# First query, key and value slabs of a two-layer decoder trunk as seven block products in Strassen's way

## The chip, the cores and the metric

The kernel runs on one core of a Trainium2 chip. The core has a matrix engine (TensorE, PE in the profile; its weight loads are shown as PEld), a vector engine (VectorE, DVE), an activation engine (ScalarE, ACT), a general engine (GpSimd, POOL) and a sync engine (SyncE, SP) that issues most DMAs. Each engine takes its instructions in the order in which they stand in its queue and waits where one is not ready. The metric is the device time of one launch in microseconds; less is better.

## The reference

Two layers on 512 tokens of 1024 channels, all float32. Layer 0 is a convolution module, layer 1 differential attention; each is followed by a gated feed-forward part (`ffn`) and a per-layer-embedding gate (`ple`). The part that matters here is the start of layer 1:

```python
h = h + sigmoid(rms_norm(h, ple_norm_g) @ ple_w_gate) * (p @ ple_w_proj)   # in substance; end of layer 0
u = rms_norm(h, attn_norm_g)
qkv = u @ w_qkv                                  # [512,1024] @ [1024,3072]
q, k, v = jnp.split(qkv, 3, axis=-1)
q = rms_norm(q.reshape(B, S, N_HEADS, 2, HEAD_DIM), q_g) * (HEAD_DIM ** -0.5)
k = rms_norm(k.reshape(B, S, N_HEADS, 2, HEAD_DIM), k_g)
...
logits = jnp.einsum('bhcqd,bhckd->bhcqk', q_blk, k) + bias[None, :, None]
probs = softmax(where(dist >= 0, logits, -inf))
w = probs[:, :, 0] - lam * probs[:, :, 1]
o = w @ v
```

`bias` is a table of 32 values for each of 8 heads, looked up by distance (T5), and `lam` one number made of four short vectors.

## The kernel before

**Arithmetic.** A float32 product is made of three passes in a reduced format: each operand is split in a high part (`hi`, a cast on ACT) and what is left (`lo`, a subtraction on DVE or POOL), and `mm3` (L166 to L170) issues lo x hi, hi x hi and hi x lo into one accumulator. `weight` (L147 ff) loads one [128 x 1024] piece of weights by SP (tile `wraw`, 2 buffers), casts it on ACT (L161, tile `whi`) and subtracts on DVE (L163, tile `wlo`). Accumulators `mm` have 4 buffers in PSUM, `sc` (scores) 2, `tp` (transposes and small things) 2.

**Order.** The program is written in stages; the instructions of each engine are set in order by a scheduler, except where a region is put under a manual schedule: there the engine's instructions stand as the code has them. `issue_after` holds an instruction behind another one in the order.

**`ple`, the end of layer 0** (L1110 to L1135). Eight products (`sums`), each one 1024 x 128 weight piece times the 512 tokens: 24 matmuls of 128x512. The first two come ahead of the normaliser: `norm.diagonal` transposes the sum of squares on PE (L237), reduces on DVE (L198, L279), takes the power on POOL (L281), and multiplies the result into two diagonal matrices on DVE (L244, L245, L286). `norm.rows` spreads them over all rows on PE (L302) and copies the outcome to `rb` on ACT (L252). Then `gate` runs for each product: accumulator times `rb` on DVE (L1122), sigmoid on ACT (L1123), times `pp` and plus `h` on DVE (L1124, L1125), and `after` for that channel group, which is `Norm.chunk`: the split of `h` times the attention norm's gain into hi (ACT, L202) and lo (DVE, L203), tiles `A0` to `A7`, and the square (ACT, L222/L225) that POOL adds to `acc` (L226). The normaliser of attention itself is applied behind the matmuls, by a factor for each token, `rcol`.

**The bias table and lambda** (L1155 to L1182). `rl` and `oh` are loaded, two matmuls (L1164) give the table by distance, DVE copies it (L1165), an ACT-queue DMA stores it to DRAM (`scr`, L1167); `bias` loads a head's rows back on the same queue (L1171). Lambda is made from a few small instructions.

**Queries, keys and values.** The weight matrix is cut into six slabs of [1024 x 512] in the order of the table `QKV` (L87): four with the queries and keys of two heads each ("q") and two with the values of four heads ("v"). A slab has four weight pieces and four token blocks of 128; `tokens` (L1200) makes one token block with 8 channel groups x 3 = 24 matmuls of 128x512, the tokens as the stationary operand. So a slab has 96. For a "q" block `unit` follows: square and copy with `rcol` on ACT (L1233, L1234), reduce on DVE (L1236), two small steps and a multiply on POOL (L1239 to L1242); and a block later `unit_end`: four transposes on PE (L1248), copies on ACT (L1256, L1257), on POOL (L1261) and on DVE (L1264, L1266) into the tiles `C0` to `C5` that the scores read. `rcol` itself is made behind the first token block (L1208 to L1210). A "v" block is an ACT copy (L1226).

**Attention blocks.** Each head has four blocks of 128 queries, each in three stages: `stage_s` (scores of two components: matmuls L1297 and L1300, an added bias with a running minimum on DVE L1310, exponentials on ACT L1314, a combination on DVE), `stage_t` (transposes L1327) and `stage_a` (the product with the values L1340). `take` hands out as many as the third entry of the `QKV` row says, to be run between the matmuls of the later slabs. Four instructions of the value slab's loop store `h` to DRAM (`rest`, SP), and `pfeatures` and the first piece of the next `ple`'s projection weights are fetched in the first query slab.

Of the kernel before, what the change touches and what calls it, by code (L numbers as in the profile page):

```python
# [12 lines left out]
F32 = mybir.dt.float32  # L13
# [7 lines left out]
P = 128  # L21
# [65 lines left out]
QKV = (("q", 0, (0, 0, 0, 0)), ("v", 0, (1, 1, 1, 2)), ("q", 1, (1, 1, 1, 2)), ("q", 2, (1, 1, 2, 1)), ("v", 1, (1, 1, 2, 2)), ("q", 3, (1, 1, 1, 1)))  # L87
# [5 lines left out]
def trunk(ctx, tc, xT, xtok, pT, wts, diag, dww, vec, rel, onehot, lamv, out):  # L93
# [29 lines left out]
    def col(name, i=0):  # L123
        a, _ = VEC[name]
        return vt[:, a + i : a + i + 1]
# [1025 lines left out]
    ple(n2, pp, lambda m, cut: norm.chunk(m))  # L1151

# [13 lines left out]

    def bias(hd):
        b = sb([P, S], "bias", 2)  # L1170
        nc.scalar.dma_start(b, bass.AP(scr.tensor, scr.offset + hd * RW, [[1, P], [1, S]]))  # L1171
        return b
# [6 lines left out]
    V.tensor_reduce(out=lam[:, 0:2], in_=lv[:, 0:2], op=ALU.add, axis=AX.X)  # L1179
# [19 lines left out]

    def tokens(ws, tb, between=()):  # L1200
# [6 lines left out]
        if rcol[0] is None:  # L1207
            r = sb([P, 4], "rcol", 1)  # L1208
            V.tensor_copy(r, norm.columns())
            rcol[0] = r  # L1210
        return acc, rcol[0][:, tb : tb + 1]
# [11 lines left out]

    def unit(pair, ws, tb, between):

        if tb == 0:  # L1226
            qk[pair] = [sb([P, 2, S], f"C{i}", 2, F32R) for i in range(6)]

            for c in range(2):
                with tc.issue_after(n2.last.ins):  # L1230
                    G.memset(f(qk[pair][4 + c][HALVES[1 - c]]), 0.0)
        acc, r = tokens(ws, tb, between)
        q, sq = big(), wk()  # L1233
# [6 lines left out]
        G.tensor_tensor(rs, rs, mhalf, ALU.pow)  # L1240
        q3 = q.rearrange("p (g d) -> p g d", g=8)
        G.tensor_tensor(q3, q3, rs.unsqueeze(2).to_broadcast([P, 8, DH]), ALU.mult)  # L1242
        return pair, tb, q
# [133 lines left out]
    todo = [(hd, qb) for hd in range(NH) for qb in range(4)]  # L1377
    todo.append(todo.pop(todo.index((NH - 2, 3))))
# [23 lines left out]
    waiting = None  # L1402
    for what, at, pace in QKV:
        ws = slab(GLO if at > 0 else 0)
        for tb in range(4):
            between = take(pace[tb])
            between += [None] * (6 - len(between))
            if waiting:
                between.append(partial(unit_end, *waiting))
                waiting = None  # L1410
            if what == "v":
                values(at, ws, tb, between)
            else:
                waiting = unit(at, ws, tb, between)

            if (what, at, tb) == ("q", 0, 1):
                ph = pfeatures(1, [both(sb([P, 2, S], t, 1, F32R)) for t in ("B4", "B5")])
            elif (what, at, tb) == ("q", 0, 2):
# [4 lines left out]

            elif (what, at) == ("v", 0):
                for c in (2 * tb, 2 * tb + 1):
                    nc.sync.dma_start(rest[c], h[c])
# [9 lines left out]
    unit_end(*waiting)  # L1436
# [204 lines left out]
```

## Time and profile before

| | |
|---|---|
| median of three runs | 1237.09 us (1237.03 to 1237.67) |
| the profiled execution's own time | 1234.18 us |
| its span | 1232.3 us |
| granted clock of PE, mean | 1.0 |
| weights read | 159 loads of 512 KB by SP, 3.6 us each from issue to landing |
| span of `ple` and the first two slabs | 542.5 to 630.7 us |

The profile shows one execution. A row of its timeline has the start in us from the span's start, the duration in us, the engine, the line of the kernel, the operation, what it writes and reads, the shape, and how many such instructions run together; in brackets stands how long the engine was idle before it and what released it. A row without a bracket followed its predecessor at once or nearly so. A row with "q" behind the engine's name is a DMA issued on that engine's queue. In the windows, each row gives a stretch and each engine's busy time in it.

### The profile page before, as it was taken

What the parts mean: (1) busy time and instruction counts of PE and PEld (TensorE: products, weight loads), DVE (VectorE), ACT (ScalarE), POOL (GpSimd) and SP (SyncE); (2) the same over time, 40 slices, a digit from 0 to 9 for tenths busy, and PEclk for the clock granted to TensorE, in tenths of its full rate; (3) what the DMA queues carried; (4) which work ended last, traced back from release to release, by engine and by line L of the source; (5) the groups of instructions that cost most, each with busy time, mean ns of one, the idle gap of its engine ahead of it and who ended that gap; (6) DMA issues with size and microseconds to landing.
All of it is one profiled execution on the core that took longest, in us unless ns stands there. A gap on an engine that the chain in (4) does not pass through costs nothing.

```text
span 1232.3 us, 18295 instructions
## 1 busy us (share of the span) xinstructions
PE 1221.3 (99%) x7003; PEld 1071.1 (87%) x7003; DVE 876.0 (71%) x1254; ACT 629.4 (51%) x1107; POOL 483.5 (39%) x360
## 2 busy tenths in 40 slices
PE   9999999999999999999999999999999999999998
PEld 7888688889998899888788888888889998999887
DVE  5979866975895488547767876747956885587545
ACT  7564554533553355435667877744524552355432
POOL 1777722025560554143436635131026641562220
PEclk9999999999999999999999999999999999999999
DMA  8484233233333232334423331243243233233321
GB/s 325 147 306 158 70 92 101 90 111 120 87 102 120 89 102 71 101 105 155 140 85 106 94 97 32 75 131 89 87 132 104 86 120 109 83 101 89 105 97 69
DMA packets 49875, 138.18 MB, mean 112 GB/s; under 512 B 5715, under 2 KB 10835, under 8 KB 49788
## 3 DMA queue, kind: packets, MB, share of 16 engines
q1 hardware_dynamic: 47520, 133.45, 33.6%
q10 hardware_dynamic: 2268, 3.57, 0.9%
q8 instruction: 55, 0.90, 0.3%
q14 instruction: 32, 0.26, 0.1%
HBM read 130.68 MB, written 6.31 MB: 111 GB/s over the span
## 4 chain that ended last, share of the span: by engine, by line
PE 92%; DVE 3%; DMA 2%; ACT 1%; issue 1%; POOL 0%; SPq 0%; ACTq 0%; DVEq 0%; POOLq 0%
PE mm L168 28%; PE mm L169 28%; PE mm L170 28%; PE mm L1340 1%; PE sc L496 1%; DVE sc L554 1%; DMA wraw<-in_wts 1%; PE sc L1300 1%; PE tp L1327 1%; PE sc L1297 1%; PE tp L1248 1%; DMA h<-in_xT 0%; DVE wlo L163 0%; DMA po<-big 0%; PE tp L1370 0%
## 5 line engine op out<-in xcount | busy, mean ns | idle before, releaser
L161 ACT CAST whi<-wraw 128x1024 fp32r<-128x1024 f32 (+1 forms) x139 | 141.2, 1025 | 230.3 <-PE mm L170 107.3
L163 DVE TENSOR_TENSOR wlo<-wraw,whi 128x1024 fp32r<-128x1024 f32 (+1 forms) x130 | 164.3, 1269 | 62.7 <-ACT whi L161 62.3
L168 PE MATMUL mm<-A,wlo 128*128 128x512 f32 (+1 forms) x524 | 203.1, 388 | 1.3 <-DVE wlo L163 1.2
L169 PE MATMUL mm<-A,whi 128*128 128x512 f32 (+1 forms) x524 | 202.4, 386 | 0.0
L170 PE MATMUL mm<-A,whi 128*128 128x512 f32 (+1 forms) x524 | 198.9, 386 | 0.0
L168 PE MATMUL mm<-B,wlo 128*128 128x512 f32 x356 | 139.0, 390 | 0.0
L169 PE MATMUL mm<-B,whi 128*128 128x512 f32 x356 | 138.8, 390 | 0.0
L226 POOL TENSOR_TENSOR acc<-acc,wk 128x512 f32<-128x512 f32 x35 | 61.1, 1744 | 195.2 <-ACT wk L225 170.8
L170 PE MATMUL mm<-B,whi 128*128 128x512 f32 x356 | 137.4, 389 | 0.0
L169 PE MATMUL mm<-C,whi 128*128 128x256 f32 (+1 forms) x450 | 127.6, 283 | 0.0
L170 PE MATMUL mm<-C,whi 128*128 128x256 f32 (+1 forms) x450 | 127.5, 283 | 0.0
L168 PE MATMUL mm<-C,wlo 128*128 128x256 f32 (+1 forms) x450 | 127.5, 283 | 0.0
L921 DVE TENSOR_TENSOR wlo<-A,whi 128x1024 fp32r<-128x1024 f32 x60 | 107.3, 1797 | 19.4 <-ACT whi L920 19.2
L168 PEld LDWEIGHTS mm<-A,wlo 128*128 128x128 f32 x524 | 98.4, 188 | 21.9 <-DVE wlo L163 1.6
L170 PEld LDWEIGHTS mm<-A,whi 128*128 128x128 f32 x524 | 98.4, 188 | 20.0
L169 PEld LDWEIGHTS mm<-A,whi 128*128 128x128 f32 x524 | 98.5, 188 | 19.6
L920 ACT CAST whi<-A 128x1024 fp32r<-128x1024 f32 x60 | 62.8, 1047 | 56.0 <-PE mm L170 45.1
L930 POOL TENSOR_TENSOR A<-A 128x512 f32<-128x512 f32 x16 | 25.8, 1614 | 161.5 <-DMA A<-in_wts 155.8
L930 POOL TENSOR_TENSOR A<-wraw 128x512 f32<-128x512 f32 x16 | 23.1, 1443 | 166.2 <-DMA wraw<-in_wts 128.7
L168 PEld LDWEIGHTS mm<-C,wlo 128*128 128x128 f32 x450 | 86.4, 192 | 0.2
L169 PEld LDWEIGHTS mm<-C,whi 128*128 128x128 f32 x450 | 86.4, 192 | 0.2
L170 PEld LDWEIGHTS mm<-C,whi 128*128 128x128 f32 x450 | 86.4, 192 | 0.1
(388 smaller groups left out, 3109.9 us busy)
## 6 DMA issues: line engine op xcount, KB each, us to landing
wraw<-in_wts SPq DMA_DIRECT2D x159, 512.0 KB, 3.6
A<-in_wts SPq DMA_DIRECT2D x32, 512.0 KB, 3.6
wraw<-in_wts SPq DMA_DIRECT2D x16, 384.0 KB, 3.0
D<-in_diag SPq DMA_DIRECT2D x17, 256.0 KB, 5.2
C<-in_diag SPq DMA_DIRECT2D x16, 256.0 KB, 5.5
h<-in_xT SPq DMA_DIRECT2D x8, 256.0 KB, 4.5
B<-in_xtok SPq DMA_DIRECT2D x4, 512.0 KB, 7.0
rest<-h SPq DMA_DIRECT2D x8, 256.0 KB, 2.0
```

The source lines that it names most:

```text
L161: A.copy(hi[:, cut], raw[:, cut])
L163: eng.tensor_tensor(lo[:, cut], raw[:, cut], f(hi[:, cut]), ALU.subtract)
L168: T.matmul(acc, al, bh, start=first, stop=False, **kw)
L169: T.matmul(acc, ah, bh, start=False, stop=False, **kw)
L170: return T.matmul(acc, ah, bl, start=False, stop=last, **kw)
L226: self.last = self.eng.tensor_tensor(self.acc, self.acc, sq, ALU.add)
L496: last_tap[0] = T.matmul(acc[:, g * P : (g + 1) * P], w, ups[c][:, g, LEAD - m : LEAD - m + P], start=(m == 0), stop=(m == LAGS - 1),)
L554: last = V.scalar_tensor_tensor(sum_, tap(j), wt(c, j), sum_, ALU.mult, ALU.add)
L920: A.copy(hi, src)
L921: V.tensor_tensor(lo, src, f(hi), ALU.subtract)
L930: G.tensor_tensor(s[:, 0], r1[:, 0], r1[:, 1], ALU.add)
L1248: turned[0] = T.transpose(t[:, i * P : (i + 1) * P], q[:, i * P : (i + 1) * P], ident)
```

## The change

The first query slab and the first value slab are made together. With the tokens cut in two halves, the channels in two halves (k = 0 to 3 and 4 to 7) and the weights of the two slabs as columns, the product of two 2x2 block matrices takes seven block products instead of eight (Strassen's scheme in Winograd's form). The blocks of the tokens are A11, A12, A22 (parts of the tiles `A0` to `A7`) and four sums S1 to S4 of blocks; those of the weights are W11, W12, W21, W22 and sums. Each block product has two token blocks x 4 channel groups x 3 matmuls of 128x512 = 24, so seven make 168 where two slabs had 192.

- `token_sums` makes S1 to S4 for channel groups k and k + 4 from `h` times the gain, while `ple` runs, as channels 4 to 7 become ready: on POOL for the first three, on DVE for the last; hi and lo on ACT and DVE.
- `sums_of` makes the sums of weight blocks on POOL (128x1024 each, 8 of them); `form` casts a block or sum and subtracts its lo part on DVE.
- `block_pair` runs the products with PE under a manual schedule, combines them (U2, P1 and P5 in tiles `D0` to `D5`), and calls `unit_norm` and `unit_end` for the query blocks and the first attention blocks in the last two products.
- The bias table's matmuls and the first steps of lambda stand ahead of `ple` in the program instead of behind it. The stores of `h` to `rest` come before the block products; `pfeatures` and the projection weight move to the next query slab.
- The first eight attention blocks have another order, since the first half of the tokens is ready first.

```diff
-QKV = (("q", 0, (0, 0, 0, 0)), ("v", 0, (1, 1, 1, 2)), ("q", 1, (1, 1, 1, 2)), ("q", 2, (1, 1, 2, 1)), ("v", 1, (1, 1, 2, 2)), ("q", 3, (1, 1, 1, 1)))
+QKV = (("q", 0, ()), ("v", 0, ()), ("q", 1, (1, 1, 2, 2)), ("q", 2, (1, 1, 2, 1)), ("v", 1, (1, 1, 2, 2)), ("q", 3, (1, 1, 1, 1)))
...
-    ple(n2, pp, lambda m, cut: norm.chunk(m))
+    def token_sums(k, eng):
+        g1, g2 = col("attn_g", k), col("attn_g", k + 4)
+        u2 = big()
+        A.activation(u2, h[k + 4], AF.Copy, scale=g2)
+        t = sb([P, 4, HT], f"B{k % 2}", 1)
+        if eng is V:
+            V.scalar_tensor_tensor(t[:, 0], h[k][:, HT:], g1, u2[:, HT:], ALU.mult, ALU.add)
+            V.scalar_tensor_tensor(t[:, 1], h[k][:, :HT], g1, t[:, 0], ALU.mult, ALU.subtract)
+        else:
+            u1 = big()
+            A.activation(u1, h[k], AF.Copy, scale=g1)
+            G.tensor_tensor(t[:, 0], u1[:, HT:], u2[:, HT:], ALU.add)
+            G.tensor_tensor(t[:, 1], u1[:, :HT], t[:, 0], ALU.subtract)
+        last_sums[k] = eng.tensor_tensor(
+            t[:, 2:4], t[:, 1:2].to_broadcast([P, 2, HT]), u2.rearrange("p (j t) -> p j t", j=2), ALU.add)
...
+        for i, (hi, lo) in enumerate(parts):
+            last_mixed[0] = A.copy(hi, t[:, i * n : (i + 1) * n])
+        for i, (hi, lo) in enumerate(parts):
+            last_mixed[1] = V.tensor_tensor(lo, t[:, i * n : (i + 1) * n], f(hi), ALU.subtract)
...
+    def after_gate(m, cut):
+        norm.chunk(m)
+        if m > 3:
+            token_sums(m - 4, G if m < 7 else V)
+        at = {0: ("11", SLABS, ("B2", "B3")), 2: ("12", SLABS + 4, ("B6", "B7")), 3: ("21", SLABS + 2, ("B4", "B5"))}
+        if m in at:
+            n, i, tags = at[m]
+            load_block(n, i, [(t, 1) for t in tags])
+        if m == 2:
+            form("1", W["11"], homes=[("C2", "C3"), ("C0", "C1")])
+        if m == 3:
+            with tc.issue_after(last_pow[0].ins):
+                sums_of(W["11"], W["12"], W["11"], ALU.subtract)
...
+    def sums_of(out, a, b, op):
+        for o, x, y_ in zip(out, a, b):
+            G.tensor_tensor(o, x, y_, op)
...
+    ple(n2, pp, after_gate)
+    load_block("22", SLABS + 6, [("wraw", 2)] * 2)
...
+    for i, at in enumerate([(0, 0), (0, 1), (1, 0), (1, 1), (0, 2), (0, 3), (1, 2), (1, 3)]):
+        todo[i] = at
...
+        for c in range(NC):
+            nc.sync.dma_start(rest[c], h[c])
...
+        for j in range(2):
+            product(a[j], "A11", "1", j, True)
+            with tc.issue_after(last_mixed[0].ins):
+                A.copy(p1[j], a[j])
+        open_pair(0)
+        form("2", W["21"])
+        products(x, "A12", "2")
+        for j in range(2):
+            with tc.issue_after(last_mixed[1].ins):
+                V.tensor_tensor(p1[j], x[j], p1[j], ALU.add)
+        form("5", W["11"])
+        with tc.issue_after(last_sums[2].ins):
+            sums_of(W["11"], W["11"], W["22"], ALU.subtract)
+        with tc.issue_after(norm.last.ins):
+            sums_of(W["12"], W["22"], W["12"], ALU.subtract)
+        products(y_, "S1", "5", factors)
+        for j in range(2):
+            waiting.append(unit_norm(0, j, p1[j], r(j)))
+        for j in range(2):
+            p5.append(sb([P, S], f"D{2 + j}", 1))
+            A.activation(p5[j], y_[j], AF.Copy, scale=r(2 + j))
+        form("6", W["11"])
+        with tc.issue_after(last_q[0].ins):
+            sums_of(W["11"], W["11"], W["21"], ALU.add)
+        for j in range(2):
+            product(a[j], "S2", "6", j, False)
+            u2.append(sb([P, S], f"D{4 + j}", 1))
+            A.activation(u2[j], a[j], AF.Copy, scale=r(j))
+        form("3", W["22"], (last_r[0], last_r[0]))
+        val[0, 0] = sb([P, 2, S], "B0", 1)
+        two = ends()
+        for j in range(2):
+            product(y_[j], "S4", "3", j, False, [None, two[j]])
+            V.scalar_tensor_tensor(val[0, 0][:, j], y_[j], r(j), u2[j], ALU.mult, ALU.add)
+        form("7", W["12"])
+        val[0, 1] = sb([P, 2, S], "B1", 1)
+        for j in range(2):
+            product(a[j], "S3", "7", j, False, take(1))
+            V.scalar_tensor_tensor(val[0, 1][:, j], a[j], r(2 + j), p5[j], ALU.mult, ALU.add)
+        form("4", W["11"])
+        for j in range(2):
+            product(a[j], "A22", "4", j, False, take(1))
+            waiting.append(unit_norm(0, 2 + j, a[j], r(2 + j)))
+
+    with tc.manual_schedule(engines={T.engine}):
+        block_pair()
+    for what, at, pace in QKV[2:]:
...
```

`products` issues channel groups 0 to 2 of both token blocks first, then `then` (here `factors`, which makes `rcol`), then group 3 of both. The changed kernel's lines of interest: scores L1385 and L1388, minimum L1398, exponential L1402, `unit_end` transposes L1336, its passes on ACT L1344 and L1345, on POOL L1349, on DVE L1352 and L1354, query scaling on POOL L1327, L1328 and L1330, value combinations L1573 and L1578.

**Where instructions move: PE in `ple`.** PE's queue in the fourth product of `ple` before: the two spread matmuls (L302, into `tp`) stand among the first matmuls of the product into `mm_5254`.

```order
L168 MATMUL mm_5254<-A_768_4859,wlo_5250 128x512
L169 MATMUL mm_5254<-A_768_4859,whi_5249 128x512
L302 MATMUL tp_5181<-wk_5145,ones_70 128x512
L170 MATMUL mm_5254<-A_768_4859,whi_5249 128x512
L168 MATMUL mm_5254<-A_770_4865,wlo_5250 128x512
L302 MATMUL tp_5181<-wk_5147,ones_70 128x512
L169 MATMUL mm_5254<-A_770_4865,whi_5249 128x512
```

The same place in the changed kernel, at the end of the fourth product (`mm_5288`); the fifth is `mm_5336`.

```order
L168 MATMUL mm_5288<-A_806_5093,wlo_5284 128x512
L169 MATMUL mm_5288<-A_806_5093,whi_5283 128x512
L170 MATMUL mm_5288<-A_806_5093,whi_5283 128x512
L302 MATMUL tp_5199<-wk_5163,ones_70 128x512
L302 MATMUL tp_5199<-wk_5165,ones_70 128x512
L168 MATMUL mm_5336<-A_768_4859,wlo_5332 128x512
L169 MATMUL mm_5336<-A_768_4859,whi_5331 128x512
```

The spread has moved behind the fourth product's last matmul, directly ahead of the fifth product, whose accumulator is the buffer that the first gate reads. The transposes ahead of it (L237) have moved from 36 matmuls into `ple` to 77.

**ACT's queue in `ple`.** In the changed kernel the store of the bias table (`scr`) and two loads from it stand among the casts of weights (`whi`), ahead of the copy to `rb`; before, they stood behind all of `ple`.

```order
L161 CAST whi_5385<-wraw_5384 128x1024
L1237 DMA scr<-C_810_5104 8x640
L1252 DMA bias_5837<-scr 128x512
L161 CAST whi_5439<-wraw_5438 128x1024
L1252 DMA bias_5902<-scr 128x512
L161 CAST whi_5493<-wraw_5492 128x1024
L252 COPY rb_5198<-tp_5199 128x512
L1123 ACT_TABLE_LOAD
```

Three DMA issues, two of which wait for the one before them, have come between the casts; the lo parts of those casts stand on DVE ahead of the reduce of the normaliser.

**POOL's queue behind `ple`.** In the changed kernel, from the last token sum (L1169) to the first query scaling:

```order
L1169 TENSOR_TENSOR B_894_5482<-B_894_5482,big_5480 128x512
L1223 TENSOR_TENSOR B_835_5213<-B_835_5213,wraw_5548 128x1024
L1223 TENSOR_TENSOR B_836_5215<-B_836_5215,wraw_5550 128x1024
L1311 MEMSET C_925_5613 64x1024
L1311 MEMSET C_926_5614 64x1024
L226 TENSOR_TENSOR acc_5211<-acc_5211,wk_5531 128x512
L1223 TENSOR_TENSOR B_847_5270<-wraw_5548,B_847_5270 128x1024
L1223 TENSOR_TENSOR B_848_5272<-wraw_5550,B_848_5272 128x1024
L281 TENSOR_TENSOR r_939_5691<-v_938_5689,mhalf_71 128x4
L1327 TENSOR_TENSOR r_942_5704<-r_942_5704,mhalf_71 128x8
```

Four weight sums now stand between the channels' last work and the power (L281) that `rcol` needs; before, that power followed the last accumulation at once.

**PE at the first scores.** In the changed kernel, both components of the first attention block (`sc_5840`):

```order
L170 MATMUL mm_5575<-wlo_5826,C_872_5380 128x512
L1385 MATMUL sc_5840<-C_923_5611,C_921_5609 128x128
L1388 MATMUL sc_5840<-C_925_5613,C_921_5609 128x128
L1385 MATMUL sc_5840<-C_924_5612,C_922_5610 128x128
L1388 MATMUL sc_5840<-C_926_5614,C_922_5610 128x128
L168 MATMUL mm_5575<-whi_5825,C_885_5435 128x512
```

Before, more than twenty matmuls of the query slabs stood between the first and the second component of that block; now they adjoin.

More of the change, by code (lines that the diff above doesn't have):

```diff
@@ new lines, in trunk, with form @@
+    forms = {}
+    def form(n, src, after=None, homes=None):
+        forms[n] = []
+        for i, raw in enumerate(src):
+            hi, lo = (
+                sb([P, 1024], tag, 2 if homes else 4, F32R) for tag in (homes[i] if homes else ("whi", "wlo")))
+            with tc.issue_after(after[0].ins) if after else nullcontext():
+                A.copy(hi, raw)
+            with tc.issue_after(after[1].ins) if after else nullcontext():
+                V.tensor_tensor(lo, raw, f(hi), ALU.subtract)
+            forms[n] += [(hi[:, j * S : (j + 1) * S], lo[:, j * S : (j + 1) * S]) for j in range(2)]
@@ L1167, in trunk @@
     nc.scalar.dma_start(scr, brow)
[L1169 to L1172, printed above, removed]
     lv = wk(F32, (P, 4, DH))
@@ L1198, in slab, with factors @@
         ]
+    last_r = [None]
+    def factors():
+        if rcol[0] is None:
+            r = sb([P, 4], "rcol", 1)
+            last_r[0] = V.tensor_copy(r, norm.columns())
+            rcol[0] = r
     def tokens(ws, tb, between=()):
@@ L1206, in tokens @@
                 between[k]()
[L1207 to L1210, printed above, removed]
         return acc, rcol[0][:, tb : tb + 1]
@@ L1222, in trunk, with open_pair, unit_norm @@
     qk = {}
+    last_q = [None]
+    def open_pair(pair):
+        qk[pair] = [sb([P, 2, S], f"C{i}", 2, F32R) for i in range(6)]
+        for c in range(2):
+            with tc.issue_after(n2.last.ins):
+                G.memset(f(qk[pair][4 + c][HALVES[1 - c]]), 0.0)
     def unit(pair, ws, tb, between):
         if tb == 0:
[L1227 to L1231, printed above, removed]
+            open_pair(pair)
         acc, r = tokens(ws, tb, between)
+        return unit_norm(pair, tb, acc, r)
+    def unit_norm(pair, tb, acc, r):
         q, sq = big(), wk()
@@ L1435, in trunk @@
                 wnext[0] = PROJ1 + 4
-    unit_end(*waiting)
+    for end in ends():
+        end()
     done, steps = [0], [0]
```

81 lines of the change are left out of this document (68 added, 13 removed).

## Prediction

> **What bounds the kernel now.** I read the profile page from the top: busy shares, then the chain that ended last, then the groups; after that the table of windows over the stage that the change rewrites, then the timeline of that stage engine by engine, looking for what TensorE (PE) waits for.
>
> ```profile
> span 1232.3 us, 18295 instructions
> PE 1221.3 (99%) x7003; PEld 1071.1 (87%) x7003; DVE 876.0 (71%) x1254; ACT 629.4 (51%) x1107; POOL 483.5 (39%) x360
> ...
> PE 92%; DVE 3%; DMA 2%; ACT 1%; issue 1%; POOL 0%; SPq 0%; ACTq 0%; DVEq 0%; POOLq 0%
> ```
>
> PE is busy 99% of the span and holds 92% of the chain: a matmul taken out is worth its full time, and any wait put on PE costs its full time. There is almost nothing to win by shortening another engine, and a lot to lose by making PE wait for one.
>
> ```profile
> 542.50:564.70 22.20, 22.20 (x101) 18.38 (x100) 10.97 (x17) 8.90 (x11) 5.60 (x5) 1.00 0.30 96
> 564.70:587.20 22.50, 22.50 (x101) 18.61 (x100) 19.75 (x24) 13.22 (x21) 9.43 (x5) 1.00 0.47 157
> 587.20:630.70 43.50, 43.50 (x205) 35.17 (x204) 29.29 (x54) 25.76 (x49) 22.34 (x24) 1.00 0.36 119
> ```
>
> The columns are length, then busy time of PE, PEld, DVE, ACT and POOL, the granted clock, DMA share and GB/s. The windows are the first and the second half of the per-layer-embedding stage (`ple`) and the first query and value slabs. PE fills each of them to the last hundredth at a clock of 1.00. So the stage that is rewritten has no wait on PE to remove. DVE is busy 60.0 of these 88.2 us, ACT 47.9, POOL 37.4.
>
> **What the change removes.** Two slabs of 96 matmuls of 128x512 become seven products of 24: 192 become 168. Nothing else that PE runs changes in number; the program has 24 fewer such matmuls, so the change does do that part of what it says.
>
> ```profile
> 537.51 0.69 DVE L1091 TENSOR_TENSOR h<-mm,h 128x512 f32<-128x512 f32 x1 [2.42 <-PE mm L170]
> ...
> 542.95 0.69 DVE L1091 TENSOR_TENSOR h<-mm,h 128x512 f32<-128x512 f32 x1 [2.42 <-PE mm L170]
> ...
> L168 PE MATMUL mm<-whi,A 128*128 128x512 f32 x192 | 76.5, 399 | 0.0
> ```
>
> Two evictions of consecutive 24-matmul products are 5.44 us apart, 0.2267 us a matmul (the 399 ns of one record overlap their neighbours, so that row's 76.5 us overstate what 192 of them take on PE: 192 x 0.2267 = 43.5). Gain: 24 x 0.2267 = **-5.44 us**, 0.44%.
>
> **What it adds elsewhere** is looked at place by place: where PE, whose order in the block part is now written out by hand, stands in front of something late. T is time on PE's own pace.
>
> **Place 1: the spread of the normaliser in `ple`.** The rel/onehot matmuls, their copies, the store to DRAM and the loads of `bias` now run inside `ple`.
>
> ```profile
> 550.91 0.60 PE L237 MATMUL tp<-ident,acc 128*128 128x128 f32 x4
> 551.55 0.69 DVE L198 TENSOR_REDUCE r<-tp 128x4 f32<-128x512 f32 x1 [5.58 <-PE tp L237]
> 553.60 1.02 POOL L281 TENSOR_TENSOR r<-v,mhalf 128x4 f32<-128x4 f32 x1 [3.58 <-DVE v L279]
> 554.94 0.69 DVE L286 TENSOR_TENSOR wk<-ident,r 128x512 fp32r<-128x512 f32 x1
> 560.01 0.39 PE L302 MATMUL tp<-wk,ones 128*128 128x512 f32 x1
> 560.88 1.22 DVE L163 TENSOR_TENSOR wlo<-wraw,whi 128x1024 fp32r<-128x1024 f32 x1 [3.52 <-ACT whi L161]
> 561.12 0.59 ACT L252 COPY rb<-tp 128x512 f32<-128x512 f32 x1 [0.26 <-PE tp L302]
> 562.03 1.28 DVE L1122 TENSOR_TENSOR big<-mm,rb 128x512 f32<-128x512 f32 x2
> 587.64 1.06 ACT L161 CAST whi<-wraw 128x1024 fp32r<-128x1024 f32 x1
> 595.46 1.24 PE L1164 MATMUL tp<-C,big 33*8 33x320 f32 x4
> 596.36 0.87 DVE L1165 COPY C<-tp 8x320 f32<-8x320 f32 x2
> 597.26 0.29 ACTq L1167 DMA_DIRECT2D scr<-C  x1
> 600.52 0.35 ACTq L1171 DMA_DIRECT2D bias<-scr  x1
> ```
>
> Before, the transposes came after 36 of `ple`'s matmuls and the spread (L302) in the fourth product, with 21 matmuls behind it to cover the copy to `rb` and the first gate. Now: `ple` begins at 542.5 (the last eviction ahead of it is the 542.95 row). After 58 matmuls, at 555.7, come the bias matmuls, 1.24 us, then 19 matmuls, the transposes at about 561.3, 19 more, and the spread, wanted at 566.1. Against it stands one queue on ACT and one on DVE: the second `C` copy, behind a new 1.22 us lo pass, at 558.5; the store of `scr` is issued, and the load of `bias` behind it on ACT's queue waits 600.52 - 597.26 = 3.26 us for it: 561.8, issue 0.35; ACT's cast 1.06 (563.2); its lo pass 1.22 on DVE (564.4), which stands ahead of the reduce 0.69 (565.1); the small step and POOL's power 1.3 (566.5); DVE's cast and two diagonal products 1.7 (568.1); second spread 0.39, copy to `rb` 0.59, gate 0.64: 569.8. The spread is now the last thing in the fourth product, and the fifth product needs the buffer that this gate frees. PE wants it at 566.5: **+3.4**. Even if the queues were all early, copy and gate alone stand bare, 0.59 + 0.64 with two hand-overs, 1.6 us. Directly behind POOL's power come two 1024-wide sums, beside DVE's diagonal products:
>
> ```profile
> 581.60 1.30 POOL L226 TENSOR_TENSOR acc<-acc,wk 128x512 f32<-128x512 f32 x1 [3.28 <-ACT wk L225]
> 634.94 2.39 POOL L163 TENSOR_TENSOR wlo<-wraw,whi 128x1024 fp32r<-128x1024 f32 x1 [4.49 <-ACT whi L161]
> 635.78 2.63 DVE L163 TENSOR_TENSOR wlo<-wraw,whi 128x1024 fp32r<-128x1024 f32 x1 [1.71 <-ACT whi L161]
> ```
>
> A lo pass of 1.22 us on DVE that began 0.84 us into POOL's 2.39 us took 2.63: it ended 1.08 us after POOL's did, as if it had stood still until then. So a POOL sum at the wrong moment can hold DVE by some 2.1 us (2.39 less a start within it). I add 2.1 once: **+5.5** in all (1.6 to 8.0, the upper end with both sums waited out, 3.4 + 2 x 2.39).
>
> The Trainium skill ("SBUF — State Buffer", section "Who interferes with whom") says the same: the port pair that DVE shares with GpSimd is an exclusive lock. These two rows agree. By it alone place 1 would be the upper end, 8.0; without it 3.4.
>
> **Place 2: the last channels reach the block products.** The eighth channel (`A` seventh) is needed 42 matmuls into the block part.
>
> ```profile
> 594.21 0.69 DVE L1125 TENSOR_TENSOR h<-h,big 128x512 f32<-128x512 f32 x1
> 595.69 0.75 DVE L203 SCALAR_TENSOR_TENSOR A<-h,vec,A 128x512 fp32r<-128x512 f32 x1 [0.19 <-ACT A L202]
> ```
>
> From the first gate to that channel DVE has 8 gates of 0.64, 8 products and 8 additions of 0.69, 8 scale-and-adds of 0.75, and seven 1024-wide passes of 1.22: 5.1 + 11.0 + 6.0 + 8.5 = 30.7 us. PE gives it 96 + 42 = 138 matmuls, 31.3 us. Full to the brim with no lock in it, and it must also stop for the end of each product. **+2.0** (0 to 5.0: two sums waited out).
>
> **Place 3: `rcol` and the first query units.** PE's order has the first query transposes 102 matmuls and the norm's transposes after `ple`, at T = 23.6 us.
>
> ```profile
> 547.17 2.85 POOL L1231 MEMSET C<- 64x1024 f32 x3
> 606.75 1.64 POOL L1240 TENSOR_TENSOR r<-r,mhalf 128x8 f32<-128x8 f32 x1
> 608.52 1.05 POOL L1242 TENSOR_TENSOR big<-big,r 128x512 f32<-128x512 f32 x1
> ```
>
> POOL ends the third token sum at about T = 6.4 (ACT's cast 1.06 and four passes of 0.6, then POOL's three, some 2.9 by the accumulation's 1.30: a full width and two halves at 0.8); then four sums 9.6, two memsets 1.9 (2.85/3 each), one accumulation 1.3: 19.2. Only then the power for `rcol`, 1.0, the copy 0.2, ACT's square 0.7, DVE's reduce 0.7, POOL's power with its addition 1.9, the multiply 1.05: 24.8 against 23.6, **+1.2** undisturbed. POOL has hardly any gap in it and each lock hit adds one to two us: I take **+2.5** (0 to 5.0).
>
> **Place 4: scores set back to back.** The scheduler used to leave matmuls between the two components of a block:
>
> ```profile
> 612.86 0.47 ACT L1256 ACTIVATE C<-tp,vec 64x256 fp32r<-64x256 f32 x1 [0.53 <-PE tp L1248]
> 614.58 0.48 DVE L1264 SCALAR_TENSOR_TENSOR C<-tp,vec,C 64x256 fp32r<-64x256 f32 x1 [0.61 <-ACT C L1257]
> 615.37 0.40 POOL L1261 CAST C<-C 64x256 fp32r<-64x256 f32 x1
> 619.53 0.22 PE L1297 MATMUL sc<-C,C 128*128 128x128 f32 x1
> 621.75 0.29 DVE L1310 CUSTOM_DVE_ANT_0 big<-sc,bias 128x128 f32<-128x128 f32 x1
> 625.02 0.22 PE L1297 MATMUL sc<-C,C 128*128 128x128 f32 x1
> ```
>
> The second component (625.02) ran 5.5 us after the first, and after DVE's minimum over the first (621.75), since both share a score tile. Now they adjoin. In the first block that minimum stands on DVE behind the value combination of the product before (0.75, from the product's end) and four passes of `unit_end` at 0.48 (L1352, L1354), then 0.29: 3.0 us after that product's end. PE has three matmuls and the first scores to run in it, 1.0 us. POOL's cast of the other component stands behind two more sums, and comes out at about 3.2. **+2.3** (2.3 to 3.4 with a lock). In the second block the same wait comes behind two lo passes, two minima with their exponentials and a combination; PE has twelve matmuls and scores, 3.4 us, for what takes 1.22 + 1.22 + 0.29 + 0.3 + 0.4 + 0.75 + 0.42 and the hand-overs, about 5.5: **+2.1** (0 to 3.0).
>
> **DVE and POOL as a whole.** DVE gets nine more 1024-wide passes, five of 512, four scale-and-adds of 512 and two of 256: 9 x 1.22 + 5 x 0.69 + 4 x 0.75 + 2 x 0.48 = 18.4 us. POOL gets eight 1024-wide sums and nine smaller ones, about 8 x 2.39 + 9 x 1.05 = 28.6. In a stretch that gets 5.4 us shorter, DVE goes from 60.0 of 88.2 us to 78.4 of 82.8. ACT's nine casts and eleven passes of 512 make 16, from 47.9 to 64: it has room.
>
> Everything else in the change costs nothing: the reordered first blocks have the same work, the early stores of `h` and the later loads for the next layer lie under a DMA share of 0.30 to 0.47.
>
> **The sum.** -5.4 + 5.5 + 2.0 + 2.5 + 2.3 + 2.1 = **+9.0 us**. The profiled execution took 1234.18 us (span 1232.3), so 1243.2 there; the median of the runs, 1237.09, is 2.9 above it: **1246**. With every low end: -5.4 + 1.6 + 0 + 0 + 2.3 + 0 = -1.5, 1235.5; with every high end +19.0, 1256.
>
> **Rivals.**
> - *The queues keep up.* One mechanism: when PE stands at place 1, all other engines gain on it, and what was late at places 2 to 4 isn't any more. Then only copy and gate remain: -5.4 + 1.6, 1233.3, faster. It decides from the point at which the queues behind place 1 have more than 4 us of slack. For it: DVE idles 11 of 22 us in the first half of `ple`. Against it: places 2 and 4 have their late work behind the gate, so it starts later too. Chance 0.10.
> - *Gain and waits cancel.* Place 1 at 3.4 and place 4's first block at 2.3, nothing else: +0.3, 1237.4. Chance 0.12.
> - *The lock cascades.* DVE at 78.4 of 82.8 us has 4.4 to spare, and eight POOL sums that each hold it for 1.4 (2.63 - 1.22) take 11. DVE becomes the bound of the stretch, each place goes to its upper end: about +17, 1254. Chance 0.20.
> - *The clock drops.* If a wait of 5 us at place 1 let PE's clock fall, the matmuls right behind would run at half speed. At 3.4 us of half speed, +1.7 for one such wait and +3.4 for two: about 1249. The rows show 1.00 throughout, PE having never waited here. Chance 0.06. The Trainium skill ("TensorE: Matmul & The Clock Gate", section "What's actually happening") gives such a rule, half the clock after an idle window of about 3.4 us; no run here shows it.
>
> **How the numbers follow.** The forecast has 0.52, its own range 1241 to 1251. Faster or slower by 0.2% is 2.5 us, about what a measurement of this kernel can tell. Faster: 0.10, the first rival. Same: 0.12, the second. Slower: 0.78, the rest. The range takes the low and high sums, 1235.5 to 1256.5; it leaves out the first rival and some of the cascade.
>
> **What would show it.** Right: PE rows right behind the second L302 wait for the gate's buffer by 2 to 8 us; the first L1385 of a second component waits for DVE's L1398; the query transposes wait for POOL; PE's busy time falls by some 5.4 us while the span grows. Wrong: PE stays at 99% through the stretch (the queues keep up), or one wait alone is above 8 us, which would be a dependence that I have not seen.

## The result and the profile after

| | before | changed |
|---|---|---|
| median | 1237.06 us (1236.35 to 1237.67, 4 runs) | 1271.51 us (1270.77 to 1275.15, 4 runs) |
| the profiled execution | 1234.18 us, span 1232.3 | 1270.77 us, span 1268.9 |
| mean granted clock | 1.0 | 0.988 |

The changed kernel is slower by 34.5 us, a ratio of 1.0285 (1.0264 to 1.0305). The sign was forecast, the size was not: 1246 was named, and 1271.5 lies well outside 1235.5 to 1256.5.

The page of the changed kernel, its span, busy times and chain:

```profile
span 1268.9 us, 18321 instructions
...
PE 1230.4 (97%) x6979; PEld 1074.0 (85%) x6979; DVE 910.9 (72%) x1274; ACT 645.0 (51%) x1128; POOL 512.4 (40%) x377
...
PE 80%; DVE 8%; ACT 4%; issue 4%; DMA 2%; POOL 2%; SPq 0%; ACTq 0%; POOLq 0%; DVEq 0%
```

PE runs the 24 matmuls less (7003 to 6979 records), and yet its busy time has grown by 9.1 us. It also idles 27.5 us more: span less busy was 11.0 and is 38.5. On the chain, PE has fallen from 92% to 80%; DVE, ACT and POOL now hold 14%.

The windows of the changed kernel (length; busy time of PE, PEld, DVE, ACT, POOL; granted clock; DMA share; GB/s) say where:

```profile
542.00:565.00 23.00, 23.00 (x103) 18.11 (x102) 11.23 (x16) 8.72 (x10) 3.10 (x2) 1.00 0.70 247
565.00:590.00 25.00, 19.30 (x73) 14.80 (x72) 20.73 (x25) 10.66 (x16) 11.46 (x7) 0.86 0.32 109
590.00:610.00 20.00, 17.24 (x68) 13.43 (x67) 17.26 (x17) 14.71 (x22) 14.08 (x11) 0.91 0.07 27
610.00:630.00 20.00, 13.14 (x49) 9.86 (x48) 19.93 (x12) 6.34 (x9) 16.29 (x9) 0.83 0.04 14
...
670.00:690.00 20.00, 16.86 (x83) 14.15 (x81) 15.23 (x28) 13.28 (x30) 11.29 (x14) 0.90 0.33 106
690.00:720.00 30.00, 29.51 (x150) 24.69 (x149) 24.37 (x57) 24.12 (x63) 17.50 (x19) 0.95 0.40 123
```

Up to 565 us nothing is lost. Then PE has holes in each window, and in five of them its clock is below 1.00. The row from 610 to 630 is the one to stop at: DVE is busy 19.93 of 20 us with only **12** instructions, 1.66 us each, where the kernel before has 27 in that window. Busy here does not mean working. The waits of PE in the same stretch (what PE was to do, who it waited for: us in total, times, longest):

```profile
PE sc L168 <- DVE A L203: 5.7, 2, 5.4
PE sc L1385 <- DVE st L1398: 4.8, 3, 2.4
PE tp L302 <- DVE wk L286: 4.2, 1, 4.2
PE tp L1415 <- ACT wth L1417: 3.0, 1, 3.0
PE mm L168 <- DVE A L203: 2.8, 2, 1.4
PE tp L1336 <- POOL big L1330: 1.9, 2, 1.2
PE mm L168 <- DVE big L1122: 1.4, 1, 1.4
PE mm L168 <- DVE wtl L1180: 1.2, 1, 1.2
PE mm L168 <- ACT D L1560: 1.1, 1, 1.1
```

They add up to 26.1 of the 27.5 us. By the places of the prediction: place 1 (L302, L1122) 5.6; place 2 (L203) 8.5, with L1180 9.7; place 3 (L1330, L1560) 3.0; place 4 (L1398) 4.8; and 3.0 at a place that was not named (L1415). From before's span to this one: -5.4 for the matmuls, +26.1 for these waits, and about +14.5 (9.1 + 5.4) because matmuls took longer. The windows' clocks lack 12 us of full speed in all (0.14 x 25 + 0.09 x 20 + 0.17 x 20 + 0.10 x 20 + 0.05 x 30), but that counts time in which PE waited: the four stretches at clock 0.50 (573.4 to 580.2, 604.1 to 607.6, 617.8 to 624.6, 686.1 to 692.9) hold 23.9 us, and PE is busy in 18.7 of them, so that the clock accounts for at most 9.4 of the 14.5. Whether that third term is a cost of its own is tried below.

Place 1 in the timeline of the changed kernel, DVE's and POOL's rows and PE's:

```profile
566.62 1.02 POOL L281 TENSOR_TENSOR r<-v,mhalf 128x4 f32<-128x4 f32 x1 [16.62 <-DVE v L279]
567.61 4.66 POOL L1223 TENSOR_TENSOR B<-B,B 128x1024 f32<-128x1024 f32 x2
...
567.67 2.33 DVE L244 CAST r<-r 128x4 fp32r<-128x4 f32 x1 [1.13 <-POOL r L281]
570.04 2.25 DVE L245 TENSOR_TENSOR v<-r,r 128x4 f32<-128x4 f32 x1
...
572.95 1.40 PE L302 MATMUL tp<-wk,ones 128*128 128x512 f32 x2 [4.20 <-DVE wk L286]
...
575.75 0.80 PE L168 MATMUL mm<-A,wlo 128*128 128x512 f32 x1 [1.40 <-DVE big L1122]
```

A cast of four columns, 0.17 us before, takes 2.33, as long as the sum on POOL beside it; the next one waits out the second sum. Place 2 in the same kernel:

```profile
612.99 5.58 POOL L1223 TENSOR_TENSOR B<-B,wraw 128x1024 f32<-128x1024 f32 x2
...
613.61 2.75 DVE L1125 TENSOR_TENSOR h<-h,big 128x512 f32<-128x512 f32 x1
616.28 3.37 DVE L1180 TENSOR_TENSOR C<-B,C 128x1024 fp32r<-128x1024 f32 x1
619.58 0.74 DVE L203 SCALAR_TENSOR_TENSOR A<-h,vec,A 128x512 fp32r<-128x512 f32 x1
620.24 6.53 DVE L1162 SCALAR_TENSOR_TENSOR B<-h,vec,big 128x256 f32<-128x256 f32 x1
...
620.37 0.79 PE L168 MATMUL sc<-whi,A 128*128 128x512 f32 x1 [5.38 <-DVE A L203]
```

The last addition to `h` (0.69 us before) takes 2.75, the lo pass behind it 3.37, and only then comes the eighth channel's L203, for which PE has stood since 615.0. These four rows are a third of the twelve instructions of that window, and hold 13.4 of its 19.93 us.

### The profile page after: what moved, and what is told of

Its sections match the earlier page's. It is cut to its first block, busy times and chain, and to the rows that moved or that the text cites. A ratio compares the mean times of both kernels' runs of the same rounds, so it can differ in the third digit from the quotient of the medians.

```text
span 1268.9 us, 18321 instructions
## 1 busy us (share of the span) xinstructions
PE 1230.4 (97%) x6979; PEld 1074.0 (85%) x6979; DVE 910.9 (72%) x1274; ACT 645.0 (51%) x1128; POOL 512.4 (40%) x377
## 3 DMA queue, kind: packets, MB, share of 16 engines
q1 hardware_dynamic: 47520, 133.45, 32.8%
## 4 chain that ended last, share of the span: by engine, by line
PE 80%; DVE 8%; ACT 4%; issue 4%; DMA 2%; POOL 2%; SPq 0%; ACTq 0%; POOLq 0%; DVEq 0%
PE mm L168 25%; PE mm L169 24%; PE mm L170 24%; PE sc L496 1%; PE mm L1428 1%; DVE sc L554 1%; DMA wraw<-in_wts 1%; POOL wk L545 1%; PE sc L1385 1%; PE sc L1388 1%; PE tp L1415 1%; ACT whi L161 1%; DVE wlo L1218 1%; PE tp L1336 0%; DVE A L203 0%
## 5 line engine op out<-in xcount | busy, mean ns | idle before, releaser
L161 ACT CAST whi<-wraw 128x1024 fp32r<-128x1024 f32 (+1 forms) x131 | 132.7, 1022 | 226.4 <-PE mm L170 109.1
L163 DVE TENSOR_TENSOR wlo<-wraw,whi 128x1024 fp32r<-128x1024 f32 (+1 forms) x122 | 152.0, 1251 | 59.7 <-ACT whi L161 59.3
```

The costliest lines, as they stand in the source:

```text
L161: A.copy(hi[:, cut], raw[:, cut])
L163: eng.tensor_tensor(lo[:, cut], raw[:, cut], f(hi[:, cut]), ALU.subtract)
```

## The experiments

Two theories at first. **L**: a POOL pass stops DVE, and the idle time that follows halves PE's clock. **O**: PE's written-out order and DVE's own load make the waits, and POOL has no part. Each comparison is with the kernel before on the same chip (1235.6 to 1236.6 us).

### No weight sums

```diff
     def sums_of(out, a, b, op):
         for o, x, y_ in zip(out, a, b):
-            G.tensor_tensor(o, x, y_, op)
+            pass
```

> Leaves out the eight sums of weight blocks on POOL (products 5, 6, 7 and 4 take plain weight blocks), all else as in the changed kernel. Theory L (a POOL sum of 2.3 us stops DVE, and PE idles long enough behind it that its clock halves): place 1 loses its 4.4 us of stopped DVE (L244 and L245 back to 0.2 us), the wait for the eighth channel at place 2 falls from 5.4 to under 2, the half-clock stretches at 580, 620 and 629 us go; about 1250 us (1245 to 1256). Rival O (PE's written-out order and DVE's own load cause the waits, POOL has no part): the waits stay, at least 1264 us.

Measured: 1257.06 us, ratio to before 1.0168 (1.0153 to 1.0183). DVE's rows at both places in e1:

```profile
566.46 0.17 DVE L244 CAST r<-r 128x4 fp32r<-128x4 f32 x1 [1.13 <-POOL r L281]
570.04 2.48 DVE L1122 TENSOR_TENSOR big<-mm,rb 128x512 f32<-128x512 f32 x4
...
606.77 1.77 DVE L1124 TENSOR_TENSOR big<-big,C 128x512 f32<-128x512 f32 x1
608.57 0.69 DVE L1125 TENSOR_TENSOR h<-h,big 128x512 f32<-128x512 f32 x1
609.18 1.22 DVE L1180 TENSOR_TENSOR C<-B,C 128x1024 fp32r<-128x1024 f32 x1
610.31 0.75 DVE L203 SCALAR_TENSOR_TENSOR A<-h,vec,A 128x512 fp32r<-128x512 f32 x1
```

The cast is back at 0.17, L1125 at 0.69, L1180 at 1.22. Theory L is right in that POOL's passes stop DVE, and the eight sums cost 14.4 us. Counted from the last addition ahead of `ple` (L1091), the first gate comes 4.0 us earlier than in the changed kernel, the last channel 8.3; the rest of the 14.4 lies behind it. The time is a microsecond above the range, and 20.5 us of loss stay without the sums: L is not all. L1124 still takes 1.77 us, where it takes 0.69 undisturbed: POOL is then at the token sums.

### The same sums on DVE, and the token sums on DVE

```diff
-            G.tensor_tensor(o, x, y_, op)
+            V.tensor_tensor(o, x, y_, op)      # e2
...
-            token_sums(m - 4, G if m < 7 else V)
+            token_sums(m - 4, V)               # e3
```

> The eight sums of weight blocks on DVE instead of POOL: DVE gets 8 x 1.22 = 9.8 us more, and loses eight stops of up to 2.3 us. Theory L: faster than the changed kernel, 1252 to 1264 us. Rival O (DVE's load is what PE waits for): slower than the changed kernel, 1272 to 1282 us.

> The token sums of channel groups 0 to 2 on DVE as those of group 3 are: DVE gets 3 x 1.65 = 5 us more, POOL loses three groups of 3.9 to 4.9 us that overlap DVE's two-input passes. Theory L: 1262 to 1270 us. Rival O: 1273 to 1278 us.

Measured: e2 1264.87 us, ratio 1.023 (1.0211 to 1.0248); e3 1269.85 us, 1.0273 (1.0257 to 1.0289). e2 is a microsecond above L's range and e3 inside it, 7 and 3 us below O's, and the gains are small: 6.6 us in e2, where taking the sums out gave 14.4, and 1.7 in e3, about as much as the runs of one kernel differ. A pass moved to DVE no longer stops it, but stands in its queue. So O is right in part: the eight sums cost 14.4 us on POOL, and still 7.8 on DVE as its own load.

### Filling the gap to keep the clock

```diff
-        products(x, "A12", "2")
+        def idle():
+            for i in range(24):
+                T.matmul(y_[0], forms["2"][0][0][:, 0:P], u[4][0], start=True, stop=True, skip_group_check=True)
+        products(x, "A12", "2", idle)
```

> Adds 24 matmuls of 128x512 without any use (into an accumulator that is free there) in front of the wait for the eighth channel, 5.4 us of PE work in a gap of 5.4 us. If the clock gate costs time of its own: PE stays at full clock behind the gap, the half-clock stretch at 620 us (6.8 us long, 3.4 us lost) goes, 1267 to 1270 us in spite of more work. If the half clock in the records costs nothing by itself: 1271 us or more.

Measured: 1271.22 us, ratio 1.0286 (1.0269 to 1.0303), as slow as the changed kernel. The windows and the waits of e4:

```profile
610.00:630.00 20.00, 17.27 (x75) 13.13 (x73) 19.41 (x12) 5.92 (x9) 15.85 (x9) 1.00 0.04 14
```

```profile
PE mm L168 <- DVE wtl L1180: 2.2, 1, 2.2
...
PE sc L168 <- DVE A L203: 0.4, 1, 0.4
```

The fill did what it was to do: the wait for the channel fell from 5.4 to 0.4 us, and the clock in that window rose from 0.83 to 1.00. The time stayed. PE reached the next thing that it needs from DVE (`wtl`, the token sums' last lo parts) the earlier, and waited there 2.2 us for 1.2. DVE is as busy as it was. So in this stretch the half clock was free: it lay inside a time that DVE sets. That is the second case of the expectation; theory L had the half clock as a cost of its own. It is shown for this stretch alone, and e4 has another one at half clock instead, between 650 and 670 us, where the changed kernel has none (clock 0.91 for 1.00).

### No sums at all

The token sums go too; the products read plain halves of `A0` to `A7`. What was held behind the token sums (the copies and additions of P1) is held behind the norm's last accumulation.

```diff
-            token_sums(m - 4, G if m < 7 else V)
+            k = m - 4
+            lo_, hi_ = slice(0, HT), slice(HT, S)
+            mixed[k] = [tuple(x[:, c] for x in norm.u[j]) for j, c in ((k, hi_), (k, lo_), (k + 4, lo_), (k + 4, hi_))]
```

> Leaves out the weight sums and the token sums with their casts and lo passes (the products take plain blocks of tokens and weights); order, bias table and attention blocks as in the changed kernel. If POOL's passes and the DVE work of the sums make the wait at place 2: no wait for a channel is left there, and of e1's 1257 us another 8 to 13 go: 1244 to 1249 us, what is left being places 1 and 4 and the clock behind them. If the forms (casts and lo passes of the products' operands) or PE's order are enough to make it: at least 1254 us.

Measured: 1249.24 us, ratio 1.0114 (1.0097 to 1.0131). The wait for channels is gone from the list. DVE's first gate and its last channel in e5:

```profile
571.39 2.48 DVE L1122 TENSOR_TENSOR big<-mm,rb 128x512 f32<-128x512 f32 x4
...
603.45 0.75 DVE L203 SCALAR_TENSOR_TENSOR A<-h,vec,A 128x512 fp32r<-128x512 f32 x1 [0.79 <-ACT A L202]
```

From the first gate to the last channel DVE takes 32.8 us here. The same measure, from the rows shown: 45.3 in the changed kernel (575.00, its first L1122, to 620.32), 41.0 in e1 (570.04 to 611.06). In these three the shorter length goes with the shorter time.

### The bias table later, the scores apart, and both without sums

```diff
     def after_gate(m, cut):
         norm.chunk(m)
+        if m == 1:
+            table()          # e6: bias matmuls, copies and store, behind the spread
...
-            product(a[j], "S3", "7", j, False, take(1))
+            product(a[j], "S3", "7", j, False, apart(take(1)) if taken[0] < LT else take(1))   # e7, and the same for "A22"
```

`apart` puts the first component behind the first channel group of the product and the second behind the fourth. In e6 the loads of `bias` are held behind the norm's last accumulation too.

> The bias table's matmuls, copies and store stand behind the spread of ple's normaliser instead of ahead of it; all else as in the changed kernel. Theory: transposes and spread come about as early as in the kernel before, PE's 5.6 us of waits at place 1 go and with them the half clock behind it; DVE's chain begins as much earlier, so the gain goes through: 1261 to 1266 us. Rival: the gain is eaten at place 2, where DVE's own load sets the time: 1269 us or more.

> In the first two attention blocks the second component's scores stand three channel groups (9 matmuls, 2.0 us) behind the first's; all else as in the changed kernel. Theory: the waits of 2.4 and 2.0 us for DVE's minimum go and nothing takes them back: 1266 to 1268.5 us. Rival: DVE's and ACT's chains behind it are as late as before, so that PE waits later for the transposed weights instead: 1270 us or more.

> All three together: no sums at all, the bias table behind the spread, the scores apart. What is left of the change is seven products for eight, their casts and PE's written-out order. If the places account for the loss: 1231.6 us and some waits at place 3, so 1232 to 1240 us. If something in the order that I have not named costs: 1245 us or more.

Measured: e6 1263.56 us, ratio 1.0226 (1.0211 to 1.0241); e7 1266.10, 1.0243 (1.0227 to 1.026); e8 1240.97, 1.0042 (1.0027 to 1.0057). The waits at place 1 are gone in e6, and its 8 us go through although place 2 follows: DVE's chain begins as much earlier. Its first gate and its last channel in e6:

```profile
564.49 1.89 DVE L1122 TENSOR_TENSOR big<-mm,rb 128x512 f32<-128x512 f32 x3
...
609.03 2.82 DVE L203 SCALAR_TENSOR_TENSOR A<-h,vec,A 128x512 fp32r<-128x512 f32 x1
```

This length is 47.4 us, longer than the changed kernel's 45.3, and e6 is faster all the same; in e2 it is 46.6. So the length alone does not order the kernels. What goes with the time better is when the last channel ends, counted from the last addition ahead of `ple`: 74.5 us in the changed kernel, 72.7 in e2, 67.4 in e6, 66.2 in e1, 58.0 in e5 and 52.8 in the kernel before.

In e7 the two waits for the minimum are gone, and 5.4 us with them. e8 came out a microsecond above its range. What PE still waits for in e8:

```profile
PE tp L1436 <- ACT wth L1438: 2.9, 1, 2.9
PE sc L1395 <- DVE st L1408: 1.6, 2, 1.3
PE mm L170 <- DVE wlo L163: 1.6, 2, 1.4
PE tp L1346 <- POOL big L1340: 0.7, 1, 0.7
...
```

The first row is the place that was not named: transposes of two attention blocks (L1415 in the changed kernel) stand next to each other at the end of a token block, and a `tp` buffer has to be emptied by ACT in between.

### What remains, and the best complete version

e9 computes everything: sums on DVE (e2), e6, e7, and another handing out of attention blocks, by which no transposes adjoin; e10 has the token sums on DVE too. e11 is e8 with that handing out. e12 is the kernel before with only the bias table and the start of lambda moved ahead of `ple`.

```diff
-("q", 1, (1, 1, 2, 2)), ("q", 2, (1, 1, 2, 1))
+("q", 1, (0, 0, 2, 2)), ("q", 2, (2, 2, 2, 1))
```

> A version that computes everything: weight sums on DVE, bias table behind the spread, scores of the first blocks apart, and the attention blocks of the third and fourth query-key slabs handed out as (0, 0, 2, 2) and (2, 2, 2, 1) so that no transposes adjoin. If the parts add: e2's 1264.9, less 8 (e6), less 5.4 (e7), less the 3 us wait of the adjoining transposes: 1246 to 1252 us. If DVE's own load at place 2 eats part of it: 1255 us or more. Slower than before in both cases.

> As e9, and the token sums of groups 0 to 2 on DVE too, so that POOL has no pass of the new sums left. If stops behind POOL still cost more than the passes on DVE: 2 to 5 us faster than e9. If DVE's load decides by now: as slow as e9 or slower.

> As e8 (no sums at all), with the attention blocks handed out as in e9. If the adjoining transposes and the half clock behind them make up e8's remainder: 1236 to 1239 us. If the remainder lies elsewhere: 1240 us or more.

> The kernel before, with one part of the change: the bias table and the first steps of lambda stand ahead of ple. Theory for place 1: the spread comes late in the fourth product and little is left to cover the copy and the first gate: 1 to 4 us slower than before, 1237 to 1240 us. Rival: without the new casts and sums in ple the queues keep up and nothing changes: within 1 us of before.

Measured: e9 1258.13 us, ratio 1.0172 (1.0157 to 1.0187); e10 1254.95, 1.0146 (1.0131 to 1.0161); e11 1239.47, 1.0022 (1.0012 to 1.0032); e12 1237.43, 1.0008 (0.9999 to 1.0018), no difference that the runs can tell, as its rival had it. e11 is half a microsecond above its range. The parts did not add in e9: 1264.9 - 8 - 5.4 - 3 would have been 1248.5, and e9 is 9.6 us above that, as the second case of its expectation had it. In e9 PE still waits 6.3 us for channels and 5.2 for the minimum; that DVE's own load at place 2 eats the gain is the likely reading, not one that was tried alone. e10 is 3.2 us faster than e9, inside the first case: with the token sums on DVE there is less to stop it. In e10, the first window behind the gate and DVE's ends:

```profile
590.00:610.00 20.00, 11.78 (x45) 8.39 (x46) 20.00 (x26) 10.87 (x16) 6.07 (x5) 0.94 0.07 26
```

```profile
564.47 1.89 DVE L1122 TENSOR_TENSOR big<-mm,rb 128x512 f32<-128x512 f32 x3
...
607.14 1.75 DVE L203 SCALAR_TENSOR_TENSOR A<-h,vec,A 128x512 fp32r<-128x512 f32 x1
```

DVE is busy 20.00 of 20 us, now with 26 instructions: for the most part working, though the last row is a pass that took 1.75 us for 0.75, beside an accumulation on POOL. Its length from first gate to last channel is 44.4 us, little less than with POOL. e10 is the best version that computes everything, and it is 18 us slower than the kernel before. Even e11, with no sums at all, does not beat it.

## Why the prediction was right in its sign and wrong in its size

| step | forecast, us | measured in the changed kernel, us |
|---|---|---|
| 24 matmuls less | -5.4 | 24 fewer records; no row contradicts 0.2267 each |
| place 1, spread and first gate | +5.5 (1.6 to 8.0) | 4.2 + 1.4 = 5.6 waited |
| place 2, last channels | +2.0 (0 to 5.0) | 13.3: 8.5 waited, 4.8 in slower matmuls; 1.2 more waited for lo parts |
| place 3, `rcol` and query units | +2.5 (0 to 5.0) | 1.1 + 1.9 = 3.0 waited |
| place 4, scores | +2.3 and +2.1 | 2.4 and 2.0 waited |
| adjoining transposes | not seen | 3.0 waited |
| half clock | nothing; a rival, 1.7 to 3.4, chance 0.06 | matmuls 14.5 longer in all, at most 9.4 by the clock, one stretch free (e4) |

- **What bounds the kernel** was right: the span grew by 36.6 us, and that is PE's 27.5 us of idle time and 9.1 of busy time. That not every wait costs its full time is what e4 shows. What the 24 matmuls are worth was not tried alone.
- **Place 1**: the mechanism was right, and that the size came out is luck. Forecast were 3.4 us without a stop and 2.1 for one; the runs show 2.2 without the sums (e1) and 3.4 more with them: DVE waited out both (2.33 and 2.25). The wait is the table, the sums and the new casts together: with the table later it goes (e6), without the sums PE waits 2.2 us for L1122 in place of 5.6 (e1's list of waits has that one row), and the table alone, in the kernel before, costs nothing that can be told (e12). My price of 1.6 us as a sure minimum was too high there: in e12 the spread does not stand last in the product.
- **Place 2 is the step that failed**, "Full to the brim with no lock in it, and it must also stop for the end of each product. +2.0 (0 to 5.0: two sums waited out)". The place was right and the term was far too small. PE had 138 matmuls there, 31.3 us, and took 44.6 for them (575.75 to 620.37): 13.3 us where the sum had 2.0, and so 11.3 of the 25.5 us by which 1246 was short. The DVE passes were counted rightly, 30.7 us between the first gate and the last channel; DVE took 45.3. Of the 14.6 us between, it stood idle for 5.5, for accumulators and for ACT's casts, and 9.2 are passes that took longer beside POOL, none of them a gate (L1122, 0.68 to 0.69 us each). By the runs, 4.3 of the 45.3 go with the weight sums (45.3 to 41.0, e1), and 8.2 with the token sums (41.0 to 32.8, e5), of which 3.7 are their three lo passes; in e5 DVE still idles 4.7. At its upper end the term let POOL stop DVE twice, behind two weight sums. In fact the token sums' passes and the accumulations on POOL did it too.
- **The lock rival** (0.20) came nearest among the rivals, at 1254: it named the right mechanism, DVE as the bound of the stretch. Its price was too low by 17.5 us, and a little below the prediction's own high ends, which add up to 19.0 (1256). The Trainium skill ("SBUF — State Buffer", section "Who interferes with whom") says that the second one to issue waits for the whole instruction; L244's 2.33 and L245's 2.25 us agree. What place 2 would have come to by that rule, used for every DVE pass with two inputs in SBUF beside every POOL pass and not for the two worst, was not worked out.
- **The clock** had no term in the sum, and its rival was priced as 3.4 us at most; the records show half-clock time in five windows. Slower matmuls outside place 2 are some 10 us, the next largest part of what the forecast lacked. But its cost can't be had by adding: e4 took one such stretch away and gained nothing. How much of the other stretches was paid for is not settled; nothing was run on them alone.
- **Place 4** was right, and its gain went through (e7, 5.4 us for 4.4 of waits). **Place 3** came out near its size, but its mechanism, the weight sums that stand on POOL ahead of the power, is not borne out: without them the query transposes still wait 1.7 of 1.9 us for POOL (e1), and 0.7 without any sums (e5).
- **What I did not look for**: a bunch of transposes in a slab behind the change, which stands in the order of the changed kernel. With it and its like undone its wait of 2.9 us is gone in e11, but the waits for the minimum are 4.0 there and 1.6 in e8; the time is 1.5 us shorter, and the two intervals (1.0027 to 1.0057 and 1.0012 to 1.0032) overlap, so the runs can hardly tell.

What stays open: e11's remainder. It is 2.8 us slower than before with 24 matmuls less, so 8 us of waits are in it. Its waits that I can name are some 5.5 us, 4.0 of them the scores of early blocks.

## What to carry to other kernels

Where PE is at 99%, a saved matmul is worth 0.23 us at most, and the vector work that saves it must find room beside what PE waits for next. Here 24 matmuls (5.4 us) were bought with eight weight sums and four token sums, which cost 22 us on the path (1271.5 to 1249.2, e5). Before such a trade, add up the vector engine's passes between the two points that PE stands at (here first gate and last channel), count each POOL pass beside a DVE pass with two inputs in SBUF as a possible stop, and compare with the matmuls in between: a stretch that came out full here, 30.7 against 31.3 us, took 45.3. And moving a pass from POOL to DVE takes the stop away and leaves the work: it helped by 6.6 us of 14.4.

## What the hardware showed beside this

- By its records, a DVE pass can be passed over by several POOL instructions in a row. The 256-wide L1162 (620.24; the one behind it took 0.48 us) took 6.53 us beside an accumulation and two sums; POOL's two sums ran at their usual 2.35 us each:

```profile
620.55 1.27 POOL L226 TENSOR_TENSOR acc<-acc,wk 128x512 f32<-128x512 f32 x1
621.78 4.71 POOL L1223 TENSOR_TENSOR B<-wraw,B 128x1024 f32<-128x1024 f32 x2
```

  It ended at 626.77, 0.28 us behind the last of them. A few microseconds earlier L1125 ended at 616.4, within a pair of sums (612.99 to 618.57): there it did get in between. So one POOL instruction is no upper end for a stop.
- Not every DVE pass is stopped: the gate L1122, which reads one input from PSUM, took its usual 0.69 us at 583.61 while POOL accumulated (581.95 to 587.1), and L1124, both inputs in SBUF, took 1.78 right behind it.

```profile
583.61 0.69 DVE L1122 TENSOR_TENSOR big<-mm,rb 128x512 f32<-128x512 f32 x1 [1.31 <-PE mm L170]
584.75 1.23 DVE L1218 TENSOR_TENSOR wlo<-B,whi 128x1024 fp32r<-128x1024 f32 x1 [0.45 <-ACT whi L1216]
585.90 1.78 DVE L1124 TENSOR_TENSOR big<-big,D 128x512 f32<-128x512 f32 x1
...
581.95 5.17 POOL L226 TENSOR_TENSOR acc<-acc,wk 128x512 f32<-128x512 f32 x3 [9.68 <-issue]
```

  It goes the other way too. L1218 has both inputs in SBUF and took its usual 1.23 us: it began at 584.75, just ahead of POOL's third accumulation (584.90), and that one took 2.23 us, where one takes 1.30 undisturbed. In these rows the one that began first ran at its usual speed.

- The clock fell without any single long gap. After two waits of 1.4 us within 4 us (599.9 to 603.6), matmuls went from 0.39 to 0.63 us a record:

```profile
601.26 0.50 PE L168 MATMUL mm<-C,A 128*128 128x512 f32 x1 [1.37 <-DVE A L203]
...
603.62 0.50 PE L168 MATMUL mm<-C,A 128*128 128x512 f32 x1 [1.39 <-DVE A L203]
...
604.67 0.63 PE L168 MATMUL mm<-C,A 128*128 128x512 f32 x1
```

  They were at 0.39 again at 607.6. The Trainium skill ("TensorE: Matmul & The Clock Gate", section "What's actually happening") names an idle window of about 3.4 us for the drop; the half-clock stretch of about 3.4 us agrees with its unit, the two gaps of 1.4 us do not make such an idle window.
